# The adaLN products of the mixers, handed out one unit behind each round of the pipelines

## The chip, the cores and the metric

The kernel runs on one core of one Trainium2 chip. The metric is device microseconds of one execution. Three runs of the kernel before gave 3426.96, 3420.39 and 3414.71 us; the median is 3420.39 us. One further execution was recorded by the profiler. All rows below come from that one.

## The reference

A trunk of four layers works on 256 latent tokens and 256 context tokens, 1024 channels each. Every layer takes six modulation vectors for each of the two streams (adaLN), from one product of a conditioning vector with a 1024 x 6144 matrix. It normalises and modulates the stream, runs two mixers side by side, projects their outputs and adds them, and then does the same with a SwiGLU.

```python
for l in range(DEPTH):
    m_l = jnp.split(cond_lat @ mod_w[l] + mod_b[l], 6, axis=-1)
    m_c = jnp.split(cond_ctx @ mod_w[l] + mod_b[l], 6, axis=-1)
    n_l = modulate(rmsnorm(h_lat, norm_mix[l]), m_l[0], m_l[1])
    ...
    h_lat = h_lat + m_l[2] * (jnp.concatenate([y1_l, y2_l], axis=-1) @ w_out[l])
    h_lat = h_lat + m_l[5] * swiglu(modulate(rmsnorm(h_lat, norm_ffn[l]), m_l[3], m_l[4]), ...)
```

Layers 0 and 2 mix with RWKV-7 (a recurrence in both directions) and a neighbourhood attention. Layers 1 and 3 mix with a gated DeltaNet (also in both directions) and an S5 state space model, whose output goes through a GELU and a gated product (`d_glu`). In the last layer the context stream is not carried on.

## The kernel before

Everything is float32. Large products are split into high and low parts and run as three matmuls of a 128 x 128 block by 512 tokens (`gemm`, L222 to L224: `pg`, `ph`, `pb` or `px <- nh, wh`). Each 256 KB piece of a weight is loaded, cast by ScalarE (`wh`, L190) and subtracted by VectorE (`wl`, L191).

**The modulation vectors.** `mod_units` is a generator. One step of it, a *unit*, loads a 512 KB block of `mod_w` (tile `mw`, two buffers, DMA issued on SP's queue at L163) and multiplies it in four matmuls, each on a quarter of the columns of TensorE (L165, `px <- mw, cnd`, 128*32). In the trace each of these is two records, so eight records are one unit. Eight units make a chunk. A chunk accumulates in the one PSUM bank of pool `x`. After the eighth unit ScalarE copies the bank (`mrow`), TensorE transposes it twice (L172), VectorE adds the bias into `mod` (L173), and only then is the bank free. There are 48 units to a layer, 192 in all: 16 ahead of layer 0, then up to 64, 112, 160 and 192 by the ends of the four layers (`MODS`). `pump(k)` runs up to k units.

**The mixers' pipeline.** `Pipe.run(i)` writes one stage of a software pipeline over eight units of work (four heads or pairs of heads, two directions): `front` for unit i, and behind it `mid` (in the odd layers `merge` and `mid`) and `rec` of the units before, by turns, in `together`. One turn of all these generators is a *round*. All of this stands at a priority of 6000 above the rest. `even_layer` calls `run` ten times, `odd_layer` eleven times; between the calls they write the input products of the layer, the attention heads, or the pieces of S5, and `pump`. In an even layer that is `pump(3)` twice for each i, in an odd one `pump(4)` twice for i = 0, 1, 2, 7, 8 and 9.

**Who else uses bank `x`.** In the odd layers `n.solo` is set, and `bank("g")` then takes its banks in turn from pools `g` and `x`. S5's outputs (L1755, `px <- s5X, s5SN` and `px <- s5T, s5U`) take `x` for every second channel tile (L1742), and the gated product (`d_glu`, L222 to L224 with `s5gh`) takes it for every second column tile. A bank of a pool goes to its takers in the order in which the program writes them.

**What sets the order.** A scheduler orders each engine's instructions at build time, by priority and by its own model of time; without a constraint it may place a unit far from where the program wrote it. Each engine then runs its queue in order. SP's queue carries all loads and stores, and each waits there for its buffer.

After the pipeline `split_y` loads the mixers' outputs again from DRAM (`yd` to `ev`, L346), the S5 half first (`ORDER`), and the output projection (`w_out`) and the SwiGLU follow. Layers 0 and 2 prepare S5's tables beside the SwiGLU.

Of the kernel before, what the change touches and what calls it, by code (L numbers as in the profile page):

```python
# [42 lines left out]
class Mixed:  # L43
    """Outputs of the mixers, channel-major, kept in DRAM by channel tile."""
# [12 lines left out]
class Net:  # L57
    def __init__(self, tc, a, ctx):
# [6 lines left out]
        # banks of PSUM by use: large products, parts of the mixers, adaLN, outputs of the mixers  # L65
# [13 lines left out]

    def load_consts(self, name, pool, tag=None, width=None):  # L80
        """A table of constants that depend on shapes alone; its parts become attributes."""
        nc = self.nc
        off, n = CONST_OFF[name]
        t = pool.tile([128, width or n], F32, name=tag or "cst_" + name)[:, :n]
        nc.sync.dma_start(t, self.a["k_" + name])
        for part, (o, w) in off.items():
            setattr(self, part, t[:, o:o + w])
# [55 lines left out]
    def mod_units(self, l, pool=None):  # L143
        """Six chunks of eight channel tiles for each stream, channel-major: [128, 48, 2].

        The weights of the first two chunks come through the pool, if one is given."""
# [9 lines left out]
        for u in range(0, 48, 8):  # L156
            if u == 16:
                pool = None
            # two units on each quarter of the partitions
# [20 lines left out]
    def unit(self, src, kt, cols):  # L180
        """src [128, kt, cols] in DRAM -> high and low tiles."""
# [12 lines left out]
    def mm3(self, out, pairs, start=True, stop=True):  # L194
        """out += sum over (lhsH, lhsL, rhsH, rhsL) of lhs.T @ rhs."""
# [7 lines left out]
    def gemm(self, W, kt, c0, cols, xh, xl, tok, done, order=None):  # L203
        """Columns c0.. of W (given as [128, kt, n]), channel-major: done(column tile, psum) for each 128."""
# [23 lines left out]
    def gemm_tok(self, W, c0, cols, xh, xl, done):  # L228
        """Columns of W, token-major: done(token tile, first column, width, psum)."""
# [21 lines left out]
    def vecs(self, pool, name, **src):  # L251
        """Vectors of multiples of 128 in DRAM, channel-major [128, n] each; they become attributes of the result."""
# [20 lines left out]
    def square_sums(self, tok):  # L273
        """Sums of h^2 over the channels, token-major: [128, token tile]."""
# [13 lines left out]
    def rstd_bcast(self, tok, ss=None):  # L288
        """1 / sqrt(mean of h^2 + eps) on all partitions: [128, tokens]."""
# [16 lines left out]
    def norm_mod(self, l, g, which, tok, ss=None):  # L306
        """nH, nL: high and low parts of the modulated RMSNorm, channel-major."""
# [124 lines left out]
def rows(x):  # L432
    """The four rows of the grid in a padded line of tokens."""
    return x[:, 1:261].rearrange("p (r w) -> p r w", w=65)[:, :, :64]


def rwkv_consts():
# [4 lines left out]
    # for a and for r, by the chunk of a tile: the mask of b on the chunk's half of the partitions, that of k on the other  # L442
# [14 lines left out]
class Rwkv:  # L457
    """Both directions of the time mixing for one layer, by pairs of heads."""
# [3 lines left out]
    def __init__(self, net, e, pool):  # L462
# [20 lines left out]
        # a of one unit, and r of three  # L483
# [7 lines left out]
    def project(self, key, i, col, nh, nl):  # L491
        """Column tile col of the input projection as tile i of a group."""
# [13 lines left out]
    def shifted(self, key, cols):  # L506
        """A group of projections, mixed with the shift of the tokens."""
# [14 lines left out]
        for i, c in enumerate(cols):  # L522
# [7 lines left out]
            else:  # L530
                # the two chunks of each tile in each other's place
# [18 lines left out]
    def tok_sums(self, prod, out):  # L550
        """out [128 tokens, tile, head] = sums over the channels of each head."""
# [4 lines left out]
    def tok_sums_swapped(self, prod, out):  # L556
        """The same, with the two chunks of each tile in each other's place."""
# [1494 lines left out]
```

## Time and profile before

| what | value |
|---|---|
| median of three runs | 3420.39 us |
| the profiled execution, first to last instruction | 3398.9 us |
| TensorE busy (matmul) | 3120.2 us, 92% |
| VectorE, ScalarE, GpSimd busy | 1920.1, 1291.6, 515.4 us |
| mean granted TensorE clock | 0.929 of full speed |
| TensorE busy with L165 (units) | 158.8 us in 1536 records |

The profiled execution's time is known as its span. The median stands 21.5 us above it, which is launch and end of the program and the difference of one run from another. Busy time of TensorE is modelled, since matmuls overlap; a wait is the idle time of an engine that a semaphore ended. "Granted clock" is the share of the full TensorE clock in a stretch.

From the first input product of a layer to its first `w_out` matmul the stretches are: layer 0 from 43.6 to 558.7 us, layer 1 from 1021.2 to 1369.5, layer 2 from 1839.7 to 2362.0, layer 3 from 2825.7 to 3141.9.

### The profile page before, as it was taken

The page shows a single profiled execution, that of the slowest core. Times are in us where ns is not written, and L with a number is a line of the kernel's source. Part 1 is how long each engine was busy: PE and PEld are TensorE (multiplying, and loading weights), DVE is VectorE, ACT ScalarE, POOL GpSimd, SP SyncE. Part 2 cuts the span into 40 slices and gives each one's busy share as a digit, 9 for nine tenths or more (in the row PEclk, how much of TensorE's full clock was granted, in tenths as well). Part 3 has the DMA queues.
Part 4 walks back from the last instruction along what each step waited for, and adds up shares of the span by engine and source line. Part 5 has one row for each costly group of instructions (what it writes and reads, how often), then busy time and mean ns, then how long its engine had stood idle before and what let it go on. Part 6 is the DMA issues. An engine that isn't in the chain of part 4 may idle for free. (4 is left out here: it accounts for less than half of the span.)

```text
span 3398.9 us, 63286 instructions
## 1 busy us (share of the span) xinstructions
PE 3120.2 (92%) x24452; PEld 2418.1 (71%) x24452; DVE 1920.1 (56%) x4229; ACT 1291.6 (38%) x2785; POOL 515.4 (15%) x1159
## 2 busy tenths in 40 slices
PE   7999789999999889899999998877999999977998
PEld 4876456787787667578887776545787777756997
DVE  3556545766436696343434556555676445685554
ACT  3334344332235335232223333434333224534444
POOL 0223310000001653000000123220000000563000
PEclk8998889999999899899998998889999999978999
DMA  8635655345345544733336634553334334644554
GB/s 282 178 97 130 151 141 156 87 136 143 111 125 143 167 126 144 245 119 94 96 100 191 184 103 128 126 125 101 102 127 136 111 113 145 196 156 156 160 176 134
DMA packets 549696, 479.21 MB, mean 141 GB/s; under 512 B 176533, under 2 KB 480531, under 8 KB 549395
## 3 DMA queue, kind: packets, MB, share of 16 engines
q1 hardware_dynamic: 549394, 475.17, 48.5%
q8 instruction: 193, 3.16, 0.4%
q14 instruction: 109, 0.89, 0.1%
HBM read 406.34 MB, written 72.90 MB: 141 GB/s over the span
## 5 line engine op out<-in xcount | busy, mean ns | idle before, releaser
L191 DVE TENSOR_TENSOR wl<-w,wh 128x512 fp32r<-128x512 f32 x786 | 545.8, 697 | 766.4 <-ACT wh L190 746.6
L190 ACT CAST wh<-w 128x512 fp32r<-128x512 f32 x786 | 484.5, 619 | 1159.7 <-PE pb L223 343.3
L222 PE MATMUL pg<-nh,wh 128*128 128x512 f32 (+2 forms) x760 | 294.6, 388 | 19.4 <-ACT nh L270 8.7
L222 PE MATMUL pb<-nh,wh 128*128 128x512 f32 (+1 forms) x832 | 305.3, 374 | 4.0 <-ACT nh L325 2.7
L223 PE MATMUL pb<-nl,wh 128*128 128x512 f32 (+1 forms) x832 | 306.5, 371 | 0.0
L224 PE MATMUL pb<-nh,wl 128*128 128x512 f32 (+1 forms) x832 | 299.8, 373 | 0.0
L223 PE MATMUL pg<-nl,wh 128*128 128x512 f32 (+2 forms) x760 | 291.4, 383 | 0.6 <-DVE gr L1179 0.6
L224 PE MATMUL pg<-nh,wl 128*128 128x512 f32 (+2 forms) x760 | 290.4, 382 | 0.1
L298 POOL TENSOR_TENSOR nr<-nv,cst_base 128x4 f32<-128x4 f32 (+1 forms) x9 | 8.4, 938 | 1660.8 <-DVE nv L296 1660.8
L222 PE MATMUL ph<-nh,wh 128*128 128x512 f32 (+1 forms) x624 | 242.0, 388 | 10.1 <-ACT nh L325 5.9
L224 PE MATMUL ph<-nh,wl 128*128 128x512 f32 (+1 forms) x624 | 240.1, 385 | 0.0
L223 PE MATMUL ph<-nl,wh 128*128 128x512 f32 (+1 forms) x624 | 239.5, 384 | 0.0
L165 PE MATMUL px<-mw,cnd 128*32 128x256 f32 x1536 | 158.8, 450 | 83.5 <-DMA mw<-in_mod_w_dram 68.9
L222 PEld LDWEIGHTS pg<-nh,wh 128*128 128x128 f32 (+1 forms) x760 | 146.3, 193 | 56.4 <-ACT nh L270 11.3
L222 PEld LDWEIGHTS pb<-nh,wh 128*128 128x128 f32 x832 | 158.6, 192 | 36.3 <-ACT nh L325 3.2
L223 PEld LDWEIGHTS pb<-nl,wh 128*128 128x128 f32 x832 | 159.5, 192 | 29.3 <-DVE nl L271 1.3
L224 PEld LDWEIGHTS pb<-nh,wl 128*128 128x128 f32 x832 | 155.5, 191 | 30.7 <-issue 1.0
L223 PEld LDWEIGHTS pg<-nl,wh 128*128 128x128 f32 (+1 forms) x760 | 146.1, 192 | 34.8 <-issue 3.0
L224 PEld LDWEIGHTS pg<-nh,wl 128*128 128x128 f32 (+1 forms) x760 | 145.7, 192 | 29.1 <-issue 1.0
L858 POOL TENSOR_TENSOR Etmp<-E 64x14 f32<-64x14 f32 (+13 forms) x448 | 160.6, 359 | 31.1
L860 POOL TENSOR_TENSOR E<-E,Etmp 64x14 f32<-64x14 f32 (+13 forms) x448 | 158.8, 354 | 32.9
L222 PEld LDWEIGHTS ph<-nh,wh 128*128 128x128 f32 x624 | 119.6, 192 | 39.7 <-ACT nh L325 6.7
(578 smaller groups left out, 6440.8 us busy)
## 6 DMA issues: line engine op xcount, KB each, us to landing
mw<-in_mod_w_dram SPq DMA_DIRECT2D x192, 512.0 KB
w<-in_f_gate_dram SPq DMA_DIRECT2D x176, 256.0 KB
w<-in_f_up_dram SPq DMA_DIRECT2D x176, 256.0 KB
w<-in_f_down_dram SPq DMA_DIRECT2D x176, 256.0 KB
w<-in_w_in_even_dram SPq DMA_DIRECT2D x104, 256.0 KB
w<-in_w_in_odd_dram SPq DMA_DIRECT2D x80, 256.0 KB
w<-in_w_out_dram SPq DMA_DIRECT2D x64, 256.0 KB
hd<-hT SPq DMA_DIRECT2D x32, 256.0 KB
```

Of the source, the lines that this page charges most:

```text
L165: nc.tensor.matmul(p[32 * c:32 * c + 32, :256], self.cnd[:, k, :], wt[:, 256 * c:256 * c + 256], start=k == 0, stop=k == KT - 1, skip_grou ...
L190: nc.scalar.copy(wh[:, :n], w[:, :n])
L191: nc.vector.tensor_tensor(wl[:, :n], w[:, :n], wh[:, :n].bitcast(F32), op=ALU.subtract)
L222: nc.tensor.matmul(o, wh[:, kk, m:m + mm], xh[:, k, tok], start=i == 0, stop=False)
L223: nc.tensor.matmul(o, wh[:, kk, m:m + mm], xl[:, k, tok], start=False, stop=False)
L224: nc.tensor.matmul(o, wl[:, kk, m:m + mm], xh[:, k, tok], start=False, stop=i == kt - 1)
L298: nc.gpsimd.tensor_tensor(r, v, self.mhalf[:, :nt], op=ALU.pow)
L858: nc.gpsimd.tensor_tensor(o, E[:, :s, s:s + 1].to_broadcast([m8, s, v]), E[:, s:s + 1, s + 1:].to_broadcast([m8, s, v]), op=ALU.mult)
L860: nc.gpsimd.tensor_tensor(E[:, :s, s + 1:], E[:, :s, s + 1:], o, op=ALU.add)
```

## The change

`together` becomes a generator that stops after each round. `Pipe` gets `pump`, and calls `pump(1)` at each stop, at the ordinary priority and behind TensorE's last instruction so far: `issue_after` gives each TensorE instruction of the unit an order (no wait) behind that one. Loads of the unit get none. The calls of `pump` in the loops of both kinds of layer go. Those behind the output projection and the SwiGLU stay, and find nothing left to do.

```diff
+    def last_pe(self):
+        return next(i for i in reversed(self.nc.cur_bb.bb.instructions) if i.engine == mybir.EngineType.PE)
...
 def together(*steps):
     while steps:
         steps = [s for s in steps if next(s, steps) is not steps]
+        yield
...
-            together(*(getattr(self.m, f)(*u(i - k), self.S[u(i - k)[0]])
-                       for k, f in enumerate(self.m.parts, 1) if u(i - k)))
+            for _ in together(*(getattr(self.m, f)(*u(i - k), self.S[u(i - k)[0]])
+                                for k, f in enumerate(self.m.parts, 1) if u(i - k))):
+                with self.n.tc.high_priority(-PRIO), self.n.tc.issue_after(self.n.last_pe()):
+                    self.pump(1)
...
         for i in range(10):
             pipe.run(i)
             go(plan.get(i, 0))
-            pump(3)
...
             for h in heads.get(i, ()):
                 na.heads(h, yt)
-            pump(3)
...
-        pumps = {0: 4, 1: 4, 2: 4, 7: 4, 8: 4, 9: 4}
...
         for i in range(11):
             pipe.run(i)
-            pump(pumps.get(i, 0))
...
             next(mix, None)
-            pump(pumps.get(i, 0))
```

The calls now fall so: in layers 0 and 2 nine in each of the stages 1 to 5 and three in stage 6; in layer 1 five, six in each of the stages 2 to 8, and one; in layer 3 five, six in each of 2 to 5, and three. No arithmetic is added or removed. In the changed file the lines stand 4 lower: L169 is L165, L176 is L172, L226 to L228 are L222 to L224, L1301, L1364 and L1759 are L1297, L1360 and L1755.

By the order of TensorE's instructions, the units that stand between the first input product of a layer and its first output projection go from 56 to 48 in layer 0, from 21 to 45 in layer 1, from 44 to 48 in layer 2 and from 24 to 32 in layer 3. Behind the first output projection of layer 1 there were 31 before layer 2's first input product (12 of them from layer 2's calls, which the scheduler had moved up); now there are 3.

Three places. The first is TensorE's queue in layer 0, where the input products run (`nh`, `wh`). Before:

```order
L222 MATMUL pg<-nh,wh 128x512
L165 MATMUL px<-mw,cnd 32x256 x4
L223 MATMUL ph<-nl,wh 128x512
L224 MATMUL ph<-nh,wl 128x512
L223 MATMUL pg<-nl,wh 128x512
L224 MATMUL pg<-nh,wl 128x512
L165 MATMUL px<-mw,cnd 32x256 x4
```

Now, at the first unit of that layer:

```order
L227 MATMUL pg<-nl,wh 128x512
L169 MATMUL px<-mw,cnd 32x256
L228 MATMUL pg<-nh,wl 128x512
L169 MATMUL px<-mw,cnd 32x256
L226 MATMUL pg<-nh,wh 128x512
L169 MATMUL px<-mw,cnd 32x256
L227 MATMUL pg<-nl,wh 128x512
L169 MATMUL px<-mw,cnd 32x256
```

A unit's four matmuls stood together; now they stand singly between input products. Of groups of L165 next to a large product there are 9 in layer 0's mixer before and 24 now, 10 and 24 in layer 2.

The second is TensorE's queue at the end of layer 1's mixer. L1297 is the pipeline's last recurrence, L1360 its last readout, `s5gh` the operand of the gated product, `pg<-nh,wh` the first output projection. Before:

```order
L222 MATMUL px<-s5gh,wh 128x512
L223 MATMUL px<-s5gl,wh 128x512
L224 MATMUL px<-s5gh,wl 128x512
L1297 MATMUL po<-gst,gRW 128x128
L1297 MATMUL pb<-gVK,gUW 128x128
L1297 MATMUL pb<-gst,gPhi 128x128
L1297 MATMUL po<-gst,gRW 128x128 x2
L165 MATMUL px<-mw,cnd 32x256 x12
L1360 MATMUL pb<-cst_base,nt 128x128 x4
L165 MATMUL px<-mw,cnd 32x256 x8
L222 MATMUL pg<-nh,wh 128x512
```

Now, from the last recurrence on:

```order
L1301 MATMUL po<-gst,gRW 128x128
L169 MATMUL px<-mw,cnd 32x256 x8
L1364 MATMUL pb<-cst_base,nt 128x128 x4
L169 MATMUL px<-mw,cnd 32x256 x8
L176 MATMUL px<-cst_base,mrow 128x128 x2
L1759 MATMUL px<-s5X,s5SN 32x8x16 x8
L1759 MATMUL px<-s5T,s5U 32x8x16 x4
```

and 14 rows further down, inside the gated product:

```order
L226 MATMUL pg<-s5gh,wh 128x512
L227 MATMUL pg<-s5gl,wh 128x512
L169 MATMUL px<-mw,cnd 32x256 x8
L228 MATMUL pg<-s5gh,wl 128x512
L169 MATMUL px<-mw,cnd 32x256 x4
L226 MATMUL pg<-s5gh,wh 128x512
L227 MATMUL pg<-s5gl,wh 128x512
L228 MATMUL pg<-s5gh,wl 128x512
L169 MATMUL px<-mw,cnd 32x256 x20
L176 MATMUL px<-cst_base,mrow 128x128 x2
L226 MATMUL px<-s5gh,wh 128x512
L227 MATMUL px<-s5gl,wh 128x512
```

Before, S5's outputs and all 48 matmuls of the gated product stood between recurrences. Now S5's last output (48 matmuls) and the whole gated product stand behind the last recurrence, with bank `x` passing from a chunk of units to S5, to a second chunk of eight units, and to the gated product. 36 of its 48 matmuls stand behind that second chunk, and five more units behind those, ahead of the first output projection.

The third is TensorE's queue at the end of layer 3's mixer. Before:

```order
L1297 MATMUL pb<-gVK,gUW 128x128
L1297 MATMUL pb<-gst,gPhi 128x128
L1297 MATMUL po<-gst,gRW 128x128 x2
L1360 MATMUL pb<-cst_base,nt 128x128 x2
L222 MATMUL pb<-nh,wh 128x256
L223 MATMUL pb<-nl,wh 128x256
```

Now:

```order
L1301 MATMUL po<-gst,gRW 128x128
L227 MATMUL px<-s5gl,wh 128x256
L228 MATMUL px<-s5gh,wl 128x256
L227 MATMUL pg<-s5gl,wh 128x256
L228 MATMUL pg<-s5gh,wl 128x256
L226 MATMUL px<-s5gh,wh 128x256
```

28 of the gated product's 48 matmuls now stand between the last recurrence and the first output projection, where there was none.

## Rows read from the trace of the kernel before

**Rows 1.** The page, its first part: busy time, share of the span, instructions.

```profile
PE 3120.2 (92%) x24452; PEld 2418.1 (71%) x24452; DVE 1920.1 (56%) x4229; ACT 1291.6 (38%) x2785; POOL 515.4 (15%) x1159
```

**Rows 2.** Busy time by stretch; columns: stretch, length, engines, clock, DMA share, GB/s.

```profile
43.60:558.70 515.10, 458.42 (x5174) 324.57 (x5175) 291.21 (x702) 211.82 (x527) 113.45 (x295) 0.89 0.57 147
1839.70:2362.00 522.30, 457.33 (x5081) 324.91 (x5077) 289.01 (x701) 210.47 (x524) 116.87 (x295) 0.89 0.50 131
1285.00:1357.00 72.00, 68.25 (x930) 53.67 (x929) 48.92 (x125) 35.61 (x85) 19.90 (x45) 0.99 0.41 131
1369.50:1830.00 460.50, 456.00 (x2126) 356.88 (x2127) 180.00 (x317) 138.12 (x239) 1.01 (x1) 0.98 0.42 131
```

**Rows 3.** The same view for L165 alone: length, PE, PEld, clock, DMA.

```profile
43.60:558.70 515.10, 48.29 (x448) 12.22 (x448) 0.89 0.57 147
1839.70:2362.00 522.30, 40.31 (x356) 10.28 (x352) 0.89 0.50 131
...
1369.50:1830.00 460.50, 20.52 (x216) 5.80 (x216) 0.98 0.42 131
```

**Rows 4.** TensorE's waits (total, times, longest): whole run; layer 0's mixer; layer 2's, two rows.

```profile
PE px L165 <- DMA mw<-in_mod_w_dram: 68.9, 48, 6.3
...
PE px L165 <- DMA mw<-in_mod_w_dram: 27.0, 17, 5.5
...
PE px L165 <- DVE mod L173: 10.2, 1, 10.2
PE px L165 <- DMA mw<-in_mod_w_dram: 6.8, 4, 6.3
```

**Rows 5.** The same pipeline stage in layers 0 and 2; wait for units in the first.

```profile
307.00:358.00 51.00, 43.10 (x560) 27.98 (x560) 33.85 (x83) 21.93 (x57) 26.78 (x61) 0.79 0.61 141
2104.00:2156.00 52.00, 47.27 (x510) 31.28 (x504) 35.91 (x86) 19.95 (x54) 23.19 (x58) 0.68 0.44 111
...
PE px L165 <- DMA mw<-in_mod_w_dram: 7.6, 4, 5.5
```

**Rows 6.** Timeline of TensorE in layer 0's input products: start, length, instruction.

```profile
95.26 0.39 PE L224 MATMUL pg<-nh,wl 128*128 128x512 f32 x1
95.58 0.62 PE L165 MATMUL px<-mw,cnd 128*32 128x256 f32 x2
...
96.46 0.40 PE L223 MATMUL ph<-nl,wh 128*128 128x512 f32 x1
96.79 0.64 PE L165 MATMUL px<-mw,cnd 128*32 128x256 f32 x8
...
97.70 0.39 PE L222 MATMUL ph<-nh,wh 128*128 128x512 f32 x1
97.93 0.39 PE L223 MATMUL ph<-nl,wh 128*128 128x512 f32 x1
```

**Rows 7.** Timeline of TensorE, end of layer 1's mixer; in brackets idle time before.

```profile
1354.77 0.39 PE L224 MATMUL px<-s5gh,wl 128*128 128x512 f32 x1
...
1356.54 0.49 PE L1297 MATMUL po<-gst,gRW 128*128 128x128 f32 x2 [0.48 <-DVE gst L1337]
...
1362.60 1.08 PE L165 MATMUL px<-mw,cnd 128*32 128x256 f32 x8 [4.46 <-DMA mw<-in_mod_w_dram]
...
1367.98 0.64 PE L165 MATMUL px<-mw,cnd 128*32 128x256 f32 x8 [2.25 <-DMA mw<-in_mod_w_dram]
1369.74 0.80 PE L222 MATMUL pg<-nh,wh 128*128 128x512 f32 x1 [1.11 <-ACT nh L270]
```

**Rows 8.** Timeline of VectorE: S5's last output in layer 1, first and last step.

```profile
1332.94 0.78 DVE L1759 STREAM_TRANSPOSE s5y<-px 128x256 f32<-128x256 f32 x2 [1.53 <-PE px L1755]
...
1342.32 0.68 DVE L271 TENSOR_TENSOR s5gl<-s5y,s5gh 128x512 fp32r<-128x512 f32 x1
```

**Rows 9.** Timeline of TensorE, end of layer 3's mixer.

```profile
3137.80 0.49 PE L1297 MATMUL po<-gst,gRW 128*128 128x128 f32 x2 [0.22 <-DVE gst L1337]
...
3142.11 0.56 PE L222 MATMUL pb<-nh,wh 128*128 128x256 f32 x1
```

More of the change, by code (lines that the diff above doesn't have):

```diff
@@ L1816, in together, with __init__ @@
         steps = [s for s in steps if next(s, steps) is not steps]
+        yield
 class Pipe:
-    def __init__(self, n, mixer, yt):
-        self.n, self.m, self.yt = n, mixer, yt
+    def __init__(self, n, mixer, yt, pump):
+        self.n, self.m, self.yt, self.pump = n, mixer, yt, pump
         self.units = [(h, d) for h in range(4) for d in range(2)]
@@ L1878, in even_layer @@
         rw.lora_in()
-        pipe = Pipe(n, rw, yt)
+        pipe = Pipe(n, rw, yt, pump)
         for i in range(10):
@@ L1949, in odd_layer @@
         n.solo = True
-        pipe = Pipe(n, gd, yt)
+        pipe = Pipe(n, gd, yt, pump)
         for i in range(11):
             pipe.run(i)
-            pump(pumps.get(i, 0))
             for _ in range(plan.get(i, 0)):
```

## The prediction, made before the changed kernel ran

> **What bounds the kernel now.** I read the page first: TensorE is busy 92% of the span [rows 1], so nearly every stage is its queue, and what a change is worth is read from where that queue stands idle or is filled with work that could hide. The second view is busy time by stretch. The mixers of layers 0 and 2 are 515.1 and 522.3 us long with TensorE busy 458.4 and 457.3 us [rows 2]; the reader is to see that some 60 us in each are idle. The projection and SwiGLU of layer 1 are 460.5 us with 456.0 busy [rows 2]: whatever stands there costs its full time. The third view is TensorE's waits. The units wait 68.9 us for their weights in all [rows 4], 27.0 us of it in layer 0's mixer, 6.8 us in layer 2's, where a unit also waits 10.2 us for the bank that VectorE still reads [rows 4]. This is the stall that one unit at a time could take away, and its upper bound is some 69 us, 2%.
>
> The question is whether those waits set the length of a mixer. Layers 0 and 2 run the same program there, and before the change they differ in the units alone: 448 records, 56 units, against 356, 44 or 45 [rows 3]. Layer 0 spends 8 us more in units [rows 3] and waits 20 us more for their weights, 10 us more if the bank's wait is counted [rows 4]. Yet it is the shorter one, by 7 us [rows 2]. One stage of the pipeline shows it closely: in layer 0 it has 7.6 us of waits for units and takes 51 us; in layer 2 no wait for a weight reaches the list, and it takes 52 us [rows 5]. So the chain through VectorE, ScalarE and the DMAs of the pipeline sets the pace, and a unit's wait mostly falls where TensorE would have waited for that chain.
>
> **Part 1: layers 0 and 2, waits taken away.** Units are spread over more of the mixer, but the last 16 of layer 0 still stand in the last hundred rows of the order, as closely as before. I count half of the waits as gone, some 13 us in layer 0 and 8 in layer 2, and by the comparison above a quarter of that on the path: 3 us each. The bounds are 0 and all of them, 27 and 17 us.
>
> **Part 2: layers 0 and 2, single matmuls.** The timeline prices an interruption of large products. Steady steps are 0.23 us apart (97.70 to 97.93). From 95.26 to 96.46 there are two such steps and one single L165 matmul (two records): 1.20 us, so the single costs 1.20 - 0.46 = 0.74. From 96.46 to 97.70 there are two steps and a whole unit: 1.24, so a whole unit costs 0.78 [rows 6]. The price is of the interruption, hardly of the work in it. Next to large products there are now 24 groups where there were 9 and 10, for about as many units: 15 more, 15 x 0.74 = 11 us in each layer. These products fill TensorE's idle time in the first half of the mixer, so not all of it is on the path; I take two thirds, 7 us, with bounds of 0 and 11. Net of part 1 it is +4 us a layer, 8 in all.
>
> The Trainium skill, "TensorEngine Tiling (Array Packing)", section Tiling Modes, says that changing the tiling mode drains the engine, which speaks against single units among full-width products; its section Performance Considerations gives a matmul about 60 cycles of overhead. By the second figure 15 more groups would cost 0.4 us a layer (an estimate, at 2.4 GHz), by the first the full price; the 0.74 us of the row agrees with the first.
>
> **Part 3: layer 1, work that leaves a full stage.** Behind the first output projection, units take 20.5 us in 216 records, 27 units [rows 3], 0.76 us each, in a stage that TensorE fills. 3 remain in place of 31 by the order, of which 27 are within this stretch: 24 fewer, 24 x 0.76 = 18, and about 1 us of waits: -19 us. This is the safest gain of the change.
>
> **Part 4: layer 1, the end of the mixer.** In the last 72 us of the mixer TensorE is 95% busy, with 68.25 us, since S5's outputs and the gated product fill the recurrence's gaps [rows 2]. They now come behind the last recurrence, because bank `x` must first be given back by a chunk of units, twice. Before, the last recurrence runs at 1356.54 and the first output projection at 1369.74: 13.2 us [rows 7]. Now, counted from the last recurrence:
> - The chunk's last four units come in two pairs. A pair of weights takes about 4.5 us, by the wait of 4.46 us behind the first pair [rows 7]: t = 9 to 10. The transposes and the addition give the bank back at 11.
> - S5's last output: 48 matmuls, some 3 us: t = 14. Its steps on VectorE and ScalarE take from 1332.94 to 1343.0, 10.1 us [rows 8]: t = 24.
> - Meanwhile the second chunk: eight units, two of them loaded ahead, three more pairs of 4.5 us from t = 15: t = 28, with the transposes and the addition 31.
> - 36 matmuls of the gated product at 0.23: t = 39.
> - From the last matmul of the gated product to the first output projection 1354.77 to 1369.74, 15.0 us [rows 7], through the gate, a store, a load and a split: t = 54. The five units hide here.
>
> So the tail grows by 54 - 13 = 41 us. The stage before it loses 48 + 48 matmuls (11 + 3 us) and takes some 12 units more (7 us): -7, fully counted since TensorE is 95% busy. Layer 1: 41 - 19 - 7 = +15 us. The tail's ends are 20 (if weights land as quickly as they are wanted, so that only S5's steps, the products and the 15 us remain beyond 13) and 50.
>
> **Part 5: layer 3.** Before, 4.3 us lie between the last recurrence and the first output projection, 3137.80 to 3142.11 [rows 9]. Now 28 matmuls of half the columns come first, 28 x 0.12 = 3.4 us, and then the way through the gate, DRAM and the split, which no longer has a recurrence to hide behind. Layer 1's 15.0 us is its upper bound, since tiles are half as large; I take 11: 3.4 + 11 - 4.3 = +10 us. Eight more units stand in the mixer, in idle time. Bounds: 0 and +14.
>
> **Sum.** +4 +4 +15 +10 = +33 us on a span of 3398.9: 3431.9. The median stands 21.5 us above that execution's span, so 3453 us.
>
> **Rivals.**
> *The waits do set the mixers' pace* (faster). For it: they are 69 us, and waits as long as 6.3 us [rows 4] stand in an in-order queue ahead of the chain's next matmul. If 60 of the 69 us go and the ends of layers 1 and 3 still cost 25, it is 3420 - 35 = 3385 us. It decides if the mixers of layers 0 and 2 both end over 15 us sooner. Against it: rows 2 to 5 above. The granted clock could help it: 0.79 in the stage with 7.6 us of waits. But it is 0.68 in the one with none [rows 5]. The Trainium skill, "TensorE: Matmul & The Clock Gate", Part 1, says that the clock follows how busy the engine has been, by which fewer waits would also give a faster clock; of these two stages that does not hold, so I add nothing for it. Chance 0.22.
>
> *Nothing in the end* (the change does little of what it says): the units in the order still come in pairs and fives, and layer 1's stage before the tail shortens by as much as the tail grows, as VectorE too is relieved of S5 (48.9 of 72 us busy [rows 2]). 3420 us, chance 0.16.
>
> *SP's queue* (slower still): loads of units wait there for a buffer that is held until a round has ended, with the pipeline's own DMAs behind them. If each of the 15 stages with units in the two odd layers loses 2 us, that is 30 more: 3483 us. Chance 0.10.
>
> **How the numbers follow.** The forecast, 3431 to 3480 us, has 0.52. A measurement of this kernel can tell about 0.3%, 10 us, from no change. Faster than that: 0.22; within: 0.16; slower: 0.52 + 0.10 = 0.62. The range from 3400 to 3490 leaves out the larger part of the first rival and a little above the last.
>
> **What would show it.** Right: layer 1's first output projection starts some 50 us behind the last recurrence (13 before); layer 3's some 15 us (4 before); the mixers of layers 0 and 2 within 10 us of their lengths; units in layer 1's SwiGLU gone, and that stage some 19 us shorter. Wrong: mixers of layers 0 and 2 shorter by over 15 us each, or a tail in layer 1 under 30 us.

## The result, and the profile after

The changed kernel takes 3517.82 us (median of four runs, 3501.86 to 3526.38), the kernel before on the same chip 3423.57 us. The ratio is 1.0269, 95% interval 1.0236 to 1.0302: about 94 us slower. The forecast was 33 us slower.

The first part of the changed kernel's page in the profile (busy time, share of the span, instructions):

```profile
PE 3160.4 (90%) x24452; PEld 2435.8 (70%) x24452; DVE 1908.0 (55%) x4229; ACT 1292.9 (37%) x2785; POOL 520.8 (15%) x1159
```

The same 24452 matmuls are busy 40 us longer than in [rows 1], and the span is 101 us longer (3500.0). So TensorE mostly waits more.

Busy time by stretch, of the changed kernel: the mixers of layers 0, 1, 2 and 3, then layer 1's output projection and SwiGLU. Columns: stretch, length, PE, PEld, DVE, ACT, POOL, granted clock, DMA share, GB/s:

```profile
44.20:593.60 549.40, 481.09 (x5109) 338.86 (x5109) 289.79 (x707) 211.70 (x526) 114.57 (x295) 0.84 0.50 131
1057.40:1467.90 410.50, 343.76 (x3104) 251.77 (x3104) 241.84 (x515) 160.98 (x366) 149.06 (x276) 0.85 0.53 158
1912.50:2450.50 538.00, 460.09 (x5109) 321.23 (x5109) 290.31 (x708) 212.62 (x527) 114.65 (x295) 0.89 0.50 129
2914.80:3240.90 326.10, 268.16 (x2677) 205.02 (x2677) 214.69 (x486) 138.23 (x328) 133.67 (x276) 0.86 0.56 166
1467.90:1912.50 444.60, 435.07 (x1939) 351.47 (x1939) 180.81 (x320) 138.04 (x238) 2.11 (x4) 0.98 0.36 108
```

Against [rows 2] and the stretches given ahead of them:

| stretch | before | after | difference | forecast |
|---|---|---|---|---|
| layer 0, mixer | 515.1 | 549.4 | +34 | +4 |
| layer 1, mixer | 348.3 | 410.5 | +62 | +34 |
| layer 1, to layer 2's first input product | 470.2 | 444.6 | -26 | -19 |
| layer 2, mixer | 522.3 | 538.0 | +16 | +4 |
| layer 3, mixer | 316.2 | 326.1 | +10 | +10 |

A second profiled execution of each kernel (e16 and e15, below) gives 517, 354, 524 and 315 us for the mixers before and 541, 419, 537 and 329 us after. So one execution tells a mixer's length to some 9 us.

TensorE's waits for weights, of the changed kernel (total, times, longest): whole run; layer 0's mixer; layer 2's; behind layer 1's last recurrence:

```profile
PE px L169 <- DMA mw<-in_mod_w_dram: 105.5, 48, 10.1
...
PE px L169 <- DMA mw<-in_mod_w_dram: 21.3, 7, 5.6
...
PE px L169 <- DMA mw<-in_mod_w_dram: 36.6, 8, 10.1
...
PE px L169 <- DMA mw<-in_mod_w_dram: 23.5, 12, 3.7
```

They went up, from 68.9 us [rows 4]. In layer 0's mixer they fell from 27.0 to 21.3 us, fewer but longer ones; in layer 2's they grew from 6.8 to 36.6 us, and 23.5 us stand behind layer 1's last recurrence.

The end of layer 1's mixer, timeline of TensorE in the changed kernel (start, length, instruction, idle time before):

```profile
1402.06 0.49 PE L1301 MATMUL po<-gst,gRW 128*128 128x128 f32 x2
...
1407.60 1.08 PE L169 MATMUL px<-mw,cnd 128*32 128x256 f32 x8 [3.21 <-DMA mw<-in_mod_w_dram]
...
1414.13 0.69 PE L176 MATMUL px<-cst_base,mrow 128*128 128x128 f32 x2 [0.49 <-ACT mrow L174]
1415.16 1.08 PE L1759 MATMUL px<-s5X,s5SN 128*32 128x128 f32 x16 [0.34 <-DVE mod L177]
...
1423.11 1.07 PE L169 MATMUL px<-mw,cnd 128*32 128x256 f32 x16
...
1428.17 0.64 PE L169 MATMUL px<-mw,cnd 128*32 128x256 f32 x8 [3.56 <-DMA mw<-in_mod_w_dram]
...
1443.49 0.80 PE L226 MATMUL px<-s5gh,wh 128*128 128x512 f32 x1 [0.34 <-DVE mod L177]
...
1452.94 0.39 PE L228 MATMUL px<-s5gh,wl 128*128 128x512 f32 x1
...
1468.13 0.79 PE L226 MATMUL pg<-nh,wh 128*128 128x512 f32 x1 [1.29 <-ACT nh L274]
```

The reader is to see the bank `px` pass from a chunk of units (to 1414) to S5 (1415), to the next chunk (1423) and to the gated product (1443), and that the first output projection stands 66.1 us behind the last recurrence, where it was 13.2 [rows 7].

What the prediction's sum leaves out is the queue that issues the loads. SP's own waits at the units' loads, in the mixers of layers 0 and 2 of the changed kernel (`px L169`: the buffer is still to be read by a unit; `mw`: an earlier load is under way):

```profile
SPq L167 <- PE px L169: 93.5, 30, 14.7
SPq L167 <- DMA mw<-in_mod_w_dram: 27.0, 6, 8.7
...
SPq L167 <- PE px L169: 72.4, 27, 12.9
SPq L167 <- DMA mw<-in_mod_w_dram: 35.3, 10, 8.6
```

and of the kernel before:

```profile
SPq L163 <- PE px L165: 71.8, 33, 7.9
SPq L163 <- DMA mw<-in_mod_w_dram: 25.3, 17, 3.1
...
SPq L163 <- PE px L165: 63.0, 24, 10.6
SPq L163 <- DMA mw<-in_mod_w_dram: 18.1, 8, 6.9
```

SP stands 120 and 108 us at these loads where it stood 97 and 81, with the mixer's other transfers queued behind. That need not be lost time: with all that it waits for, SP waits 381 us in layer 0's mixer of the changed kernel, and still 363 us in e8 below, where there are no such loads.

### The profile page after: what moved, and what is told of

It reads as the page before. It is cut to its first block, busy times and chain, and to the rows that moved or that the text cites. A ratio compares the mean times of both kernels' runs of the same rounds, so it can differ in the third digit from the quotient of the medians.

```text
span 3500.0 us, 63297 instructions
## 1 busy us (share of the span) xinstructions
PE 3160.4 (90%) x24452; PEld 2435.8 (70%) x24452; DVE 1908.0 (55%) x4229; ACT 1292.9 (37%) x2785; POOL 520.8 (15%) x1159
## 5 line engine op out<-in xcount | busy, mean ns | idle before, releaser
L226 PE MATMUL pb<-nh,wh 128*128 128x512 f32 (+1 forms) x832 | 304.7, 376 | 21.0 <-ACT nh L274 15.3
L226 PE MATMUL pg<-nh,wh 128*128 128x512 f32 (+2 forms) x760 | 298.4, 393 | 26.0 <-ACT nh L274 8.6
L228 PE MATMUL pb<-nh,wl 128*128 128x512 f32 (+1 forms) x832 | 299.3, 373 | 0.0
L228 PE MATMUL pg<-nh,wl 128*128 128x512 f32 (+2 forms) x760 | 294.6, 388 | 3.3 <-DVE wl L195 3.3
L169 PE MATMUL px<-mw,cnd 128*32 128x256 f32 x1536 | 177.7, 479 | 109.2 <-DMA mw<-in_mod_w_dram 105.5
L226 PE MATMUL ph<-nh,wh 128*128 128x512 f32 (+1 forms) x624 | 243.3, 390 | 14.4 <-ACT nh L329 5.7
L228 PE MATMUL ph<-nh,wl 128*128 128x512 f32 (+1 forms) x624 | 243.2, 390 | 1.1 <-DVE wl L195 1.1
L226 PEld LDWEIGHTS pb<-nh,wh 128*128 128x128 f32 x832 | 157.8, 192 | 54.2 <-ACT nh L274 10.7
L226 PEld LDWEIGHTS pg<-nh,wh 128*128 128x128 f32 (+1 forms) x760 | 148.0, 195 | 63.6 <-issue 10.8
L228 PEld LDWEIGHTS pb<-nh,wl 128*128 128x128 f32 x832 | 155.9, 192 | 30.8 <-DVE wl L195 1.5
L228 PEld LDWEIGHTS pg<-nh,wl 128*128 128x128 f32 (+1 forms) x760 | 147.5, 194 | 36.4 <-DVE wl L195 4.4
L169 PEld LDWEIGHTS px<-mw,cnd 128*32 128x32 f32 x1536 | 44.7, 122 | 177.4 <-DMA mw<-in_mod_w_dram 129.2
```

What stands on the lines that cost most here:

```text
L169: nc.tensor.matmul(p[32 * c:32 * c + 32, :256], self.cnd[:, k, :], wt[:, 256 * c:256 * c + 256], start=k == 0, stop=k == KT - 1, skip_grou ...
L226: nc.tensor.matmul(o, wh[:, kk, m:m + mm], xh[:, k, tok], start=i == 0, stop=False)
L228: nc.tensor.matmul(o, wl[:, kk, m:m + mm], xh[:, k, tok], start=False, stop=i == kt - 1)
```

## The experiments

Times are medians; the kernel before, run beside them, took 3414 to 3419 us. Intervals in brackets are those of the ratio to it. Mixers' lengths are from each run's trace.

### Which layers: e1, e2

```diff
-        pipe = Pipe(n, gd, yt, pump)
+        pipe = Pipe(n, gd, yt, None)
+            pump(pumps.get(i, 0))
```

(Excerpt. e1; e2 does the same to the even layers, with `pump(3)` twice.)

> The change in the even layers alone; the odd layers hand out their units as before. If each layer's mixer pays for its own order, the mixers of layers 0 and 2 keep the lengths of the changed kernel, some 549 and 538 us, those of layers 1 and 3 go back to some 349 and 316 us, and layer 1's output projection and SwiGLU, with 19 units behind it in place of 31, takes some 461 us: 3424 + 34 + 16 - 9 = 3465 us. The rival, that the loss of the even layers comes from what the odd layers leave over for them (units still due, the granted clock), gives mixers of layers 0 and 2 near 515 and 522 us and a total near 3415 us.

> The change in the odd layers alone; the even layers hand out three units at two places of each stage, as before. If each layer pays for itself, the mixers of layers 0 and 2 are 515 and 522 us, that of layer 1 some 410 us with some 55 to 66 us between its last recurrence and its first output projection, that of layer 3 some 326 us; with 24 units behind layer 1's output projection in place of 31 that stage is 5 us shorter: 3424 + 62 + 10 - 5 = 3491 us. The rival, that layer 1's loss comes with the changed layer 0 in front of it, gives a layer 1 near 349 us and 3430 us.

Measured: e1 3475 us (1.0137 to 1.0179), mixers of 546, 359, 548 and 329 us; e2 3481 us (1.0149 to 1.0196), mixers of 516, 406, 527 and 338 us. Each kind of layer pays for its own order, as the theory had it, though the two losses, 56 and 62 us, come to more than the 94 us of both together. One thing did not fit: layer 3 of e1 has the program of the kernel before and took 329 us, not 316. In the traces some 850 of its 2668 TensorE records stand in another order than before, where a second execution of the kernel before shows 46: the scheduler spreads a change into layers that it does not touch.

### Order or pace: e3, e4

```diff
-                with self.n.tc.high_priority(-PRIO), self.n.tc.issue_after(self.n.last_pe()):
+                with self.n.tc.high_priority(-PRIO):
                     self.pump(1)
```

```diff
+                self.due = getattr(self, "due", 0) + 1
+                if self.due % 3 == 0:
...
-                    self.pump(1)
+                        self.pump(3)
```

> One unit behind each round as in the changed kernel, but without the order behind TensorE's last instruction. In the queue the single matmuls between input products go from 14 to 3 and 1 in layers 0 and 2, while the tail of layer 1 keeps its sequence of units, S5 outputs and gated product. If the order is what the even layers pay for, their mixers come back to within 8 us of 515 and 522, and the total is 3424 + 62 + 10 - 6 = some 3490 us. If the pace of one unit for each round (and the loads that go with it) is the cause, the mixers stay near 549 and 538 us and the total near 3515 us.

> The order behind TensorE's last instruction is kept, but three units stand behind every third round in place of one behind each. The queue still has 13 groups of single matmuls between input products in each even layer, and the same tail in layer 1. If the order is what is paid for, lengths stay near the changed kernel's: mixers of layers 0 and 2 at 545 and 535 us or more, total some 3515 us. If it is one unit at a time that costs, the mixers of layers 0 and 2 lose most of their growth, below 525 and 530 us, and the total is near 3480 us.

Measured: e3 3498 us, layer 0's mixer 522 us as the order theory wanted, but layer 2's 546 us as its rival wanted. e4 3538 us, mixers of 569 and 537 us: three units at a time behind the same order are no better than one. In layer 0 it is the order behind TensorE's last instruction that costs, not one unit at a time; for layer 2 the two runs leave it open.

### The causes as the trace first suggested them: e5, e6, e7

In the trace the last of the first 528 input products starts 265 and 261 us into the even mixers, 239 and 240 us before the change, and between them units stand where TensorE has no idle time. e5 takes them out of there, e6 keeps chunks from standing between S5's takers of bank `x`, e7 does both.

```diff
+                if i > 2 or isinstance(self.m, Gdn):
                     with self.n.tc.high_priority(-PRIO), self.n.tc.issue_after(self.n.last_pe()):
```

```diff
+                if isinstance(self.m, Rwkv) or not 2 < i < 7 or self.n.done % 8:
                     with self.n.tc.high_priority(-PRIO), self.n.tc.issue_after(self.n.last_pe()):
```

> The changed kernel, but in the even layers the rounds of stages 1 and 2 hand out no unit, so that none stands between input products; the order behind TensorE's last instruction stays, and all 48 units stand in the rest of the mixer, more closely. Theory: the even layers lose by units that stand in the second half of the input products, where TensorE has no idle time; the products then end some 240 us into the mixer as before (264 and 261 us in the changed kernel), and the mixers take 549 - 24 = 525 us or less and 538 - 21 = 517 us: total 3518 - 45 = 3473 us. Rival: the units in the later stages are what costs (held behind a round, with waits for weights of up to 10 us); with more of them there the mixers stay at 549 and 538 us or grow, and the total is 3518 us or more.

> The changed kernel, but in the odd layers stages 3 to 6 of the pipeline only finish a chunk that is begun, so that S5's outputs and the gated product find bank x free; 22 units stand in layer 1's mixer in place of 45 and 26 behind its first output projection in place of 3. Theory: the tail of layer 1 comes from the handing over of the bank; it falls from 66 us to 15 us or less, the mixer from 411 to some 355 us, the stage behind it grows by 23 x 0.76 = 17 us to 462 us; layer 3 gains up to 8 us: total 3518 - 55 + 17 - 4 = 3476 us. Rival: the units' loads on SP's queue are what delays the end; then the tail stays above 45 us.

> Both of the limits above at once: in the even layers no unit in stages 1 and 2, in the odd ones none in stages 3 to 6 beyond a begun chunk. If the two losses have the two causes named and nothing else of size, they go independently: 3518 - 45 - 42 = 3431 us, within 0.5% of the kernel before. If something else in the change costs (the order behind TensorE's last instruction, units in single file), some 3460 us or more remain.

e5: 3517 us, mixers of 560 and 525 us. Nothing is gained in all (layer 0 lost 11 us, layer 2 gained 13). No unit stands between products any more, yet the products end at 261 and 246 us, not at the 240 that was expected: units between products are not what the even layers pay for, and that theory falls (e8 below says the same). e6: 3490 us; layer 1's mixer 361 us, its end (timeline of TensorE):

```profile
1405.51 0.49 PE L1301 MATMUL po<-gst,gRW 128*128 128x128 f32 x2
1409.18 0.64 PE L169 MATMUL px<-mw,cnd 128*32 128x256 f32 x8 [3.18 <-DMA mw<-in_mod_w_dram]
...
1418.09 0.79 PE L226 MATMUL pg<-nh,wh 128*128 128x512 f32 x1 [0.29 <-ACT nh L274]
```

12.6 us in place of 66: without the hand-over of the bank the long tail is gone. Yet it takes waits for weights as well to make it 66 us: in e8, e13 and e17 below, a chunk still hands the bank to the gated product behind the last recurrence, 36 of its matmuls and eight units follow, but no unit waits, and the tail is 20, 21 and 23 us. e7: 3509 us, with mixers of 562, 371, 556 and 321 us. The even layers' loss is still there, in full.

### The loads: e8 to e12

```diff
-                wt = (pool or self.raw).tile([128, 1024], F32, name="mw", bufs=16 if pool else 2)
-                nc.sync.dma_start(wt, W[:, k, u * 128:u * 128 + 1024])
...
+                    if not hasattr(self, "mwk"):
+                        self.mwk = self.raw.tile([128, 1024], F32, name="mwk", bufs=1)
+                        nc.sync.dma_start(self.mwk, W[:, k, u * 128:u * 128 + 1024])
+                    wt = self.mwk
```

(Excerpt. e8: from the 17th unit on all units multiply one block that is loaded once, and the other 175 loads are left out. e9 is the same edit of the kernel before. e10 issues every load as well, into one buffer `mw` that nothing reads. e11 and e12 only replace `nc.sync` by `nc.gpsimd` in the load, in the changed kernel and in the one before.)

> The changed kernel, but from unit 17 on every unit multiplies one block of adaLN weights that is loaded once; the loads of the others are left out, and with them all of the units' waits for weights (105.5 us in the changed kernel: 21 in layer 0's mixer, 37 in layer 2's, 30 in layer 1's, of which 23.5 behind the last recurrence, 13 in layer 3's). If these waits mostly lie beside the pipeline's chain, as the prediction had it, the even mixers lose less than 10 us each, layer 1's tail some 23 us, and the total is some 3518 - 45 = 3473 us. If waits for weights set the pace of the mixers, nearly all of the 105 us goes: 3415 us or less.

> The kernel before, with one resident block of weights for all units from unit 17 on and the loads of the others left out (the counterpart of the run with the changed kernel, 3389 us). Theory: loads cost the changed kernel more than the kernel before, since a unit now stands right behind a round, ahead of the next round's first matmul; then the kernel before gains only the part of its 68.9 us of waits that the comparison of layers 0 and 2 left on the path, a quarter or 17 us, and some 3400 us come out, so that without loads the change is worth nothing or a little. Rival: loads cost both kernels alike; then 3418 - 128 = some 3290 us, and the change is 100 us slower with or without them.

> The changed kernel with the resident block of weights for the products, but the loads of all units go on as well, into one buffer that nothing reads: TensorE has no wait for weights, the traffic is there. If TensorE's waits are what the loads cost (and the 128 us that the run without loads gained), this run is near it, below 3420 us. If the traffic itself costs, by standing on SP's queue and on the DMA engines ahead of the pipeline's transfers, it stays above 3480 us.

> The changed kernel, with the units' loads from unit 17 on issued by GpSimd's queue in place of SP's; traffic, buffers and products are the same. If the weights come late because their loads stand in SP's queue behind others that wait for buffers (or delay these), the waits for weights fall from 105 us to below 60 and the time to some 3460 us or less. If the length of a load on the DMA engines is what counts, nothing changes: 3518 us within 15. GpSimd, busy 15%, could also be held up by loads that wait for a buffer; then it is slower than 3518 us.

> The kernel before with the same move of the units' loads to GpSimd's queue. Its waits for weights are 68.9 us in place of 105; by the theory that SP's queue makes the weights late it gains some 10 to 20 us (3400 to 3410 us), less than the changed kernel. By the rival nothing changes: 3420 us within 10.

e8: 3389 us, ratio 0.9903 to 0.9940, so faster than the kernel before. Its mixers of layers 0 and 2 (length, PE busy, granted clock, DMA share, GB/s):

```profile
43.10:552.90 509.80, 459.92 (x5109) 0.91 0.38 91
1837.00:2346.70 509.70, 455.33 (x5109) 0.92 0.37 87
```

40 and 28 us shorter than with loads. Its products still end late, at 272 and 271 us, with as many single matmuls between them: neither sets the end of an even mixer. e9: 3421 us, ratio 0.9986 to 1.0029: without loads the kernel before gains nothing. Its mixers of layers 0 and 2:

```profile
42.90:569.40 526.50, 464.13 (x5175) 0.89 0.36 88
1851.90:2372.70 520.80, 447.35 (x4870) 0.85 0.36 85
```

So the loads cost the changed kernel 119 to 129 us (against the kernel before run beside each, or against the changed kernel's own median) and the kernel before none, and without them the change is worth some 32 us.

e10 took 3543 us (1.0346 to 1.0403), above its second theory's 3480, but told nothing between the two: unbounded, the loads ran ahead, 123 of them into layer 0's mixer, which took 608 us with SP standing at them for 337; layers 2 and 3, where none were left, took 518 and 320 us. e11: 3540 us, with mixers of 554, 415, 542 and 334 us, though TensorE's waits fell from 105.5 to 71 us; e12: 3496 us (1.0209 to 1.0260). Moving the loads to another queue makes both slower. GpSimd then waits for a buffer at these loads, 374 us in e11 and 744 us in e12. The Trainium skill, "DMA: Bandwidth & Descriptors", section Issuing engines are not separate DMA queues, says that another issuing engine only saves the time of the issue; e11 and e12 agree in that nothing is gained, but both got slower, by 22 and 82 us.

### What of the loads: e13, e14, e17

```diff
+                    wt = self.raw.tile([128, 1024], F32, name="mw", bufs=1)
+                    nc.sync.dma_start(wt, W[:, k, u * 128:u * 128 + 1024])
+                    wt = self.mwk
...
+                with self.n.tc.high_priority(-PRIO), self.n.tc.issue_after(self.n.last_pe()), self.n.tc.issue_after(self.n.last_sp()):
```

(Excerpt. e13: the products use e8's block, and each load, into a buffer that nothing reads, keeps about its place in SP's queue. e17 differs from it in one line: `wt = self.dram.tile([128, 1024], F32, name="mwd", bufs=16)`, so that the loads go to 16 buffers in DRAM. e14 has the changed kernel's two buffers and loads 64 columns in place of 1024.)

> The changed kernel with one resident block of weights for the products of the units from 17 on; the loads go on into a buffer that nothing reads, but each is ordered behind SP's last instruction at its round, so that they keep about the places in SP's queue that they have in the changed kernel. If TensorE's waits for weights are what the loads cost, this run comes to the time without loads, 3390 to 3420 us, with even mixers below 520 us. If the bytes or the places in SP's queue cost, it stays at 3480 us or more, with even mixers at 535 us or more.

> The changed kernel with loads of 32 KB in place of 512 KB for the units from 17 on (the first 64 columns of each block, which the product reads four times over): buffers, waits, queue entries and products stay. If the bytes cost, by the time that they take to land or by what they delay, the time falls to some 3400 us, and the waits for weights from 105 us to below 50. If the loads cost by when they can be issued (a load waits on SP until the unit two before it has run, and that unit stands behind a round on TensorE), waits of 60 us and more are left and the time stays above 3480 us.

> The changed kernel with one resident block of weights for the products from unit 17 on, and the loads of the units going on at the same places of SP's queue, but into 16 buffers in DRAM that nothing reads, so that neither SP nor TensorE ever waits for one. If the bytes are what slows the even mixers, they stay near 547 and 542 us and the total near 3480 us; if it is SP's queue standing at loads that wait, they come to some 510 to 520 us and the total to 3390 to 3410 us.

e13: 3482 us (1.0150 to 1.0245). TensorE's waits for weights are down to 4.2 us in all, yet the even mixers are as long as ever (windows, then SP's waits in the same two):

```profile
43.30:590.10 546.80, 473.35 (x5109) 0.87 0.51 131
1875.60:2417.50 541.90, 466.97 (x5109) 0.88 0.50 128
```

```profile
SPq L177 <- DMA mw<-in_mod_w_dram: 118.1, 42, 9.2
...
SPq L177 <- DMA mw<-in_mod_w_dram: 138.0, 42, 7.4
```

e17: 3420 us (0.9984 to 1.0038), with the same bytes on the DMA engines:

```profile
42.70:555.30 512.60, 459.51 (x5109) 0.91 0.53 140
1852.90:2378.80 525.90, 461.88 (x5109) 0.90 0.50 132
```

```profile
SPq L177 <- DMA mwd<-in_mod_w_dram: 6.8, 7, 1.4
...
SPq L177 <- DMA mwd<-in_mod_w_dram: 3.6, 4, 1.5
```

The two differ in whether a load waits in SP's queue: 118 and 138 us there, 7 and 4 us here; 34 and 16 us of the two mixers and 62 us of the whole go with it. In layer 0, 14 of the 34 us are TensorE's busy time, at a granted clock of 0.87 against 0.91. The two also differ in where the bytes land, on the chip in e13 and in DRAM in e17, which no run tells apart from the waiting. And such standing need not lengthen a mixer: in layer 1's of e13, SP stands as follows, against 2.9 us in e17, and the mixers are 379 and 383 us long.

```profile
SPq L177 <- DMA mw<-in_mod_w_dram: 95.4, 34, 5.0
```

e14: 3439 us (1.0039 to 1.0082); TensorE's waits 43.3 us, SP's 86 and 66 us, mixers of 532, 373, 523 and 324 us. It came between its theories: both kinds of wait shrank, but most of SP's stayed, and so did some 20 us.

Side by side: changed kernel 3518; without TensorE's waits 3482 (-36, in layer 1 above all: 411 to 379 us); with loads that never wait, in DRAM, 3420 (-62); without the bytes 3389 (-31). Against the kernel before run beside each, that is +94, +64, +3 and -25 us, so steps of 30, 61 and 28. The scheduler orders each of these kernels anew, so each step carries its reshuffling too.

### Again, and without order and hand-over: e15, e16, e18

```diff
+                if isinstance(self.m, Rwkv) or not 2 < i < 7 or self.n.done % 8:
-                with self.n.tc.high_priority(-PRIO), self.n.tc.issue_after(self.n.last_pe()):
+                    with self.n.tc.high_priority(-PRIO):
```

(Excerpt. e18. e15 and e16 are the changed kernel and the kernel before as they are.)

> The changed kernel once more, for a second profiled execution: mixers of layers 0 to 3 within 1% of 549, 411, 538 and 326 us if one execution is enough to read a term of 10 us from; otherwise they differ by 10 us and more with the granted clock of the stretch.

> The kernel before once more, for a second profiled execution: mixers of layers 0 to 3 within 1% of 515, 348, 522 and 316 us if one execution is enough; otherwise they differ by 10 us and more with the granted clock of the stretch.

> One unit behind each round as in the changed kernel, but without the order behind TensorE's last instruction, and in the odd layers no more than the rest of a begun chunk in stages 3 to 6. 33 units stand behind layer 1's first output projection. If order and hand-over are what the change costs, the time comes to within 15 us of the kernel before, 3420 to 3435 us, with even mixers at 515 to 530 us and layer 1's at 350 to 362. If one unit at a time costs by itself, it stays at 3455 us or more.

e15 and e16 (one run each, 3507 and 3412 us) agree with the first traces within 3 us in five of the eight mixers; layer 1 before differs by 6, the changed layers 0 and 1 by 8 and 9, where the granted clock differs too (0.84 and 0.87 in layer 0, 0.85 and 0.83 in layer 1). e18: 3436 us (1.0043 to 1.0093), mixers of 522, 368, 521 and 331 us, close to the theory's 3420 to 3435, with layer 1's mixer above its 350 to 362. With one unit behind each round, but without the order and without the hand-over of the bank, some 80 of the 94 to 100 us are gone; the order alone (e3) gave back 20 us and the hand-over alone (e6) 28.

SP's standing at units' loads and the length of the even mixers, over the runs that have both (us, layers 0 and 2):

| kernel | SP stands | mixer |
|---|---|---|
| before; again | 97, 81; 101, 82 | 515, 522; 517, 524 |
| e2, even layers as before | 73, 54 | 516, 527 |
| e3, no order | 75, 51 | 522, 546 |
| e18, no order, whole chunks | 73, 77 | 522, 521 |
| e14, small loads | 86, 66 | 532, 523 |
| e17, loads never wait | 7, 4 | 513, 526 |
| changed; again | 120, 108; 113, 106 | 549, 538; 541, 537 |
| e1; e6, even layers as changed | 128, 125; 117, 110 | 546, 548; 545, 552 |
| e4, by threes | 119, 90 | 569, 537 |
| e5; e7, behind the products | 101, 91; 101, 95 | 560, 525; 562, 556 |
| e13, unread, paced | 118, 138 | 547, 542 |

The last five rows have the order and full loads that wait: 90 to 138 us, and mixers of 525 to 569. The others: up to 101 us, and 513 to 532, but for layer 2 of e3. So the order with its loads tells the mixers apart, the standing by itself does not: e5 and e7 stand 101 us in layer 0 and take 560 and 562 us, the second execution of the kernel before stands 101 us and takes 517.

## Why the prediction was wrong

**Direction right, size a third.** It said 3453 us and 3400 to 3490; 3518 lies outside.

**The step that failed** is the sum for layers 0 and 2, +4 each, where +34 and +16 were measured: 42 of the 68 us that the profiled spans lie beyond the forecast. It counted waits taken away from TensorE and single matmuls added to it, and put the loads that move with the units at nothing. What the runs show in its place is that the new order pays for its loads: without them its even mixers take 510 and 510 us (e8), and the kernel before gains nothing without its own (e9). Loads on SP's queue stood among the rivals, but only for the two odd layers, at 2 us a stage, 30 us in all and a chance of 0.10; between e13 and e17, 50 of the 62 us are in the even mixers and none in layer 1's. A second term, layer 1 with its 15 us, was 21 us too small (part 4).

How the loads lengthen an even mixer is argued, not shown. A unit that is ordered behind a round holds its buffer until TensorE gets there, and SP's queue stands at the load two units on; e13 and e17 speak for that standing as the cost. Against it speak layer 1 of e13, e5 and e7 in the table, and the changed kernel's own queue: of its 28 stands of over 3 us in the two even mixers, the transfer directly behind had by its semaphores been ready for over half a microsecond in 3 at most.

**Part 1** (-3 in each even layer) counted 13 and 8 us of waits for weights as gone; layer 0 lost 6 of 27.0, and layer 2's grew by 30, though its wait of 10.2 us for the bank did go. Its reading that these waits lie beside the chain held for the kernel before, where e9 shows them worth nothing, and for the changed even mixers, which are as long in e13, where no unit waits. It did not hold in layer 1, whose mixer fell from 411 to 379 us without them.

**Part 2** had the right price and the wrong place. Timeline of TensorE in the changed kernel, products and singles by turns:

```profile
217.55 0.40 PE L227 MATMUL pg<-nl,wh 128*128 128x512 f32 x1
217.88 0.62 PE L169 MATMUL px<-mw,cnd 128*32 128x256 f32 x2
218.42 0.50 PE L228 MATMUL pg<-nh,wl 128*128 128x512 f32 x1
218.85 0.62 PE L169 MATMUL px<-mw,cnd 128*32 128x256 f32 x2
219.40 0.49 PE L226 MATMUL pg<-nh,wh 128*128 128x512 f32 x1
```

From product to product 0.87 and 0.98 us in place of 0.23 [rows 6]: 0.64 to 0.75 a single, as [rows 6] had it (0.74). But e8 keeps such singles and is at 510 us, and e5 takes them away and gains nothing. What is delayed in the first half of an even mixer does not set its end.

**Part 3** (-19) was right. Units behind layer 1's output projection, busy time in L169 alone (stretch, length, PE, PEld, clock, DMA):

```profile
1467.90:1912.50 444.60, 1.89 (x24) 0.52 (x24) 0.98 0.36 108
```

20.52 - 1.89 = 18.6 us less than in [rows 3]. The stage lost 26: waits for weights of 2.9 us went too, and for the rest no row accounts.

**Part 4**: the mechanism was right, and e6 shows it; two terms were wrong in size, one of them in sign. The tail was to grow from 13 to 54 us and grew to 66 (68 in the second execution). Counted from the last recurrence at 1402.06, S5 has the bank at 13 us (11 forecast), but the second chunk gives it back at 41 (31 forecast), since it starts at 21, not at 15, and its eight units take 19 us, not 13; the rest took 25 us where 23 were forecast. The stage before it was to lose 7 us and gained 9 (last recurrence 335 us into the mixer before, 345 now; 341 and 351 in the second executions), though S5's last output and the gated product left it; what holds it up isn't shown. With part 3, layer 1 was to cost 15 us and costs 36.

**Part 5** (+10) came out at +9.9. Timeline of TensorE, end of layer 3's mixer, changed kernel:

```profile
3228.84 0.43 PE L1301 MATMUL po<-gst,gRW 128*128 128x128 f32 x2
...
3233.57 0.28 PE L228 MATMUL pg<-s5gh,wl 128*128 128x256 f32 x1
3241.12 0.80 PE L226 MATMUL pb<-nh,wh 128*128 128x256 f32 x2 [7.05 <-ACT nh L274]
```

12.3 us where [rows 9] have 4.3: 8 us are shown, where the sum had 10 (the products took 4.7 us, not 3.4, and the way behind them 7.6, not 11). That the whole came out at +9.9 is luck: the second executions differ by 14, and layer 3 took 329 us in e1 with the program of before.

**The rivals.** That waits set the mixers' pace (faster) is refuted for the kernel before by e9. The new order does have a gain, but not that one: e8 is 32 us faster than e9, and in neither does a unit of the mixers wait for weights. 17 and 11 us of it are in the even mixers, 21 behind layer 1's output projection and 6 in layer 3's mixer, against 22 lost in layer 1's. Nothing had been added to the sum for the clock. It did move, and down: 0.84 of the 2.4 GHz in layer 0's mixer where it was 0.89 [rows 2], and 0.91 in e8; TensorE's busy time went with it (481, 458 and 460 us for nearly the same matmuls), so that up to some 20 of layer 0's 34 us came with a slower clock. But in the second executions TensorE is busy 464 us after (0.87) and 466 us before (0.88): there none of the 24 us came that way.

**What stays open.** Which transfer behind a load, or which engine, lengthens the even mixers isn't shown, nor whether e17 gains by not waiting or by loading into DRAM. Why layer 2 of e3 took 546 us with 51 us of standing is not known, nor what makes the last 20 us of e18. A third buffer for the weights, the plain remedy, was not tried; it would tell whether the buffers are what counts.

## What to carry to other kernels

When work is moved, price the loads that move with it too: when each buffer comes free, how long the issuing queue will stand for it, and whether what is queued behind was ready. An order that ties a unit to a place on one engine ties its load to a place on another. The cheapest test is to leave the loads out in both kernels: it showed at once that the new order was 32 us better without loads, and that its loads cost it some 120 us or more. And where a PSUM bank passes between users in program order, handing one user's work out evenly puts it between all the others: here the tail grew from 13 to 66 us.

## What the runs showed of the hardware that was not expected

With the same bytes in about the same places of the queue, loads that wait for their one buffer on the chip cost 62 us more than loads into DRAM that hardly wait (e13, e17), while no unit waited for one of them in either; the waiting and the destination are not told apart. Loads that hardly wait cost half of that, 28 to 31 us for 176 loads of 512 KB (e17 against e8), at a DMA share of 0.53 in place of 0.38 in layer 0's mixer. And GpSimd's queue, with the engine busy 15%, was a worse place for the loads than SP's, by some 20 to 35 us in the changed kernel (3540 us, 1.0368 of the kernel before, against 3518 and 1.0269) and 82 us in the kernel before; why is not shown.
